# Gate and up projections of a feed-forward layer in seven block products for each pair of weight tiles, with 1/rms moved past the down projection

## The chip, the cores and the metric

The kernel runs on one core of a Trainium2 chip. The metric is the time of one execution on the device, in microseconds; the lower the better.

## What is computed

Two layers of a decoder trunk over 512 positions of width 1024, all in float32. The change touches the second half of each layer, the gated feed-forward (D_FF is 2816), and what follows from it:

```python
h2 = rmsnorm(x, ffn_norm[layer])
gu = jnp.einsum('bsd,df->bsf', h2, w_gate_up[layer])
x = x + jnp.einsum('bsf,fd->bsd', jax.nn.silu(gu[..., :D_FF]) * gu[..., D_FF:], w_down[layer])
```

After the second layer one more `rmsnorm` with `final_norm` gives the output. The first half of each layer (one input projection, three token mixers, their gates and an output projection `w_out`) is not touched.

## The kernel before

**Tiles.** Activations are kept with channels on the 128 partitions and the 512 positions on the free axis, so the layer input is 8 tiles of 128x512 (`KT`). A weight tile of 128x1024 floats holds the 8 blocks of 128x128 that lead from all 1024 input channels to 128 output channels. To keep float32 accuracy each operand is split in a high and a low part (`wh` and `wl` for weights, `hH`, `hL` for activations) and every block takes three matmuls: high with high, high with low, low with high. `fm_tile` (line 343) does one weight tile this way: 8 blocks x 3 = 24 matmuls of 512 columns into one PSUM bank.

**Weights.** `wload` (line 203) brings one weight tile: a DMA of 512 KB on SyncE's queue into `st`, a copy on ScalarE that makes `wh`, a subtraction on VectorE that makes `wl`. `st` has two buffers, `wh` and `wl` three each. Whatever stands under `tc.high_priority()` is put ahead of other ready work on its engine.

**Norm.** `Norm.add` (line 387) takes a finished tile of x while the output projection `w_out` still runs, multiplies it by the norm's gain and splits it; the factor 1/rms per position is only known once all 8 tiles are there. `finish` (line 404) makes it: `rst` with positions on partitions, `rep` the same repeated on all partitions.

**Feed-forward** (lines 1211 to 1247). For each of 22 pairs (`KF`) of a gate tile and an up tile: two `fm_tile`s; VectorE multiplies the gate by `rep`; ScalarE takes silu; GpSimd multiplies by `rep` (for the up half); VectorE multiplies with the up bank; ScalarE copies the high part (`aH`), GpSimd subtracts the low part (`aL`). In layer 0 the down projection then runs tile by tile with `fm_acc`, and VectorE adds each bank to x. In layer 1 `last_down` (line 1259) runs it with positions on partitions and does the final norm; `residual_tm` (line 1249) turns x for that on the side, for 8 of the pairs.

**Order.** TensorE's order is the order of the program, written by hand with generators that `Issue.run` interleaves. Every other engine executes its instructions in the order in which the tile scheduler put them when the kernel was built, and an instruction that waits holds up all that stand behind it on its engine. All instructions are issued by one helper, so they carry one line number (L120 before, L121 in the changed kernel) and are told apart by their tiles.

Of the kernel before, what the change touches and what calls it, by code (L numbers as in the profile page):

```python
# [164 lines left out]
def hybrid_kernel(ctx, tc, x0, pos, wi, wkv, wb, wo, wg, wd, gn, convw, lngb, sguw, sgub,  # L165
# [267 lines left out]
    def layer(l, norm, first=None):  # L433
# [777 lines left out]
        with tc.tile_pool(name=f"ffn{l}", bufs=1, reuse_waits="tile") as fp:  # L1211
            hx = nx.xs
            issue.spawn(0, nx.finish(), nx.accs[0])
            act = []
            for i in range(KF):
                pgt = yield from fm_tile(wg[l, 2 * i], hx)
                pup = yield from fm_tile(wg[l, 2 * i + 1], hx)
                if i == 0:
                    yield f"rep{nx.gi}"
                    rep2 = nx.rep  # L1220
# [7 lines left out]
                nc.scalar.copy(ah, s)  # L1228
                nc.gpsimd.tensor_tensor(al_, s, ah.bitcast(F32), ALU.subtract)
# [183 lines left out]
```

## Time and profile before

| | |
|---|---|
| time, median of 3 runs | 1726.81 us (1724.46 to 1728.25) |
| the profiled execution: its time | 1728.58 us |
| its span, first to last instruction | 1726.5 us |
| mean granted TensorE clock | 0.996 of full speed |
| TensorE matmuls busy | 1706.7 us, 99% of the span |
| VectorE busy | 852.8 us, 49% |
| ScalarE busy | 648.0 us, 38% |
| GpSimd busy | 414.8 us, 24% |
| the chain that ended last | 95% on TensorE |

The rows below come from this profiled execution. Matmuls overlap in the pipeline, so the mean duration of one (389 ns for 512 columns) is not what one adds to the time; the distance from start to start is.

### The profile page before, as it was taken

Reading aid. Unit: us, or ns where it says so; the run is one execution under the profiler, and the core shown is the slowest. Engines: PE = TensorE matmul, PEld = TensorE weight load, DVE = VectorE, ACT = ScalarE, POOL = GpSimd, SP = SyncE. Lnnn points to the kernel's source line nnn. Section 1 sums busy time; section 2 is a strip of 40 time slices with the busy share of each in tenths; the row PEclk is TensorE's granted clock in tenths of the full one; section 3 lists DMA queues with packets and bytes.
Section 4 is the critical chain, followed back from the end, with each engine's and each line's share of the span. In section 5 each row is a group of like instructions: output and inputs, shape, how many; then the busy total and the mean of one; then the engine's idle time right before and its main releaser. Section 6 shows DMA issues by size and latency. Waiting matters only on the chain.

```text
span 1726.5 us, 22439 instructions
## 1 busy us (share of the span) xinstructions
PE 1706.7 (99%) x8580; PEld 1410.4 (82%) x8580; DVE 852.8 (49%) x1624; ACT 648.0 (38%) x1206; POOL 414.8 (24%) x457
## 2 busy tenths in 40 slices
PE   9999999999999999999999999999999999999998
PEld 8888778888888888888888877788888888888886
DVE  7685874544543333323276948644444433333224
ACT  6454663323342222222245546532233322222212
POOL 3423231021223333310024133210212233333000
PEclk9999999999999999999999999999999999999999
DMA  5232112232443223344332220122224534444332
GB/s 163 93 104 90 38 46 96 86 98 90 130 153 99 97 97 98 98 128 125 109 117 98 95 80 26 57 91 91 98 98 134 164 105 120 120 122 158 98 98 85
DMA packets 73116, 176.59 MB, mean 102 GB/s; under 512 B 24945, under 2 KB 25201, under 8 KB 73009
## 3 DMA queue, kind: packets, MB, share of 16 engines
q1 hardware_dynamic: 71184, 170.71, 31.0%
q0 software_dynamic: 1248, 3.41, 0.7%
q8 instruction: 67, 1.10, 0.3%
q10 hardware_dynamic: 576, 1.05, 0.2%
q14 instruction: 41, 0.33, 0.1%
HBM read 162.03 MB, written 13.11 MB: 101 GB/s over the span
## 4 chain that ended last, share of the span: by engine, by line
PE 95%; DVE 2%; ACT 1%; POOL 1%; issue 0%; DMA 0%; SPq 0%; POOLq 0%; ACTq 0%; DVEq 0%
PE mm L120 83%; PE px L120 12%; DVE U L120 0%; DVE wl L120 0%; DMA x<-in_x 0%; ACT pr L120 0%; POOL of L120 0%; DVE xf L120 0%; DVE pr L120 0%; DVE S L120 0%; DVE zg L120 0%; DVE Tc L120 0%; ACT wh L120 0%; POOL pr L120 0%; ACT ojk L120 0%
## 5 line engine op out<-in xcount | busy, mean ns | idle before, releaser
L120 ACT CAST wh<-st 128x1024 fp32r<-128x1024 f32 (+2 forms) x286 | 295.6, 1033 | 815.5 <-PE mm L120 611.0
L120 PE MATMUL mm<-hH,wh 128*128 128x512 f32 x1344 | 532.9, 396 | 0.0
L120 PE MATMUL mm<-hH,wl 128*128 128x512 f32 x1344 | 524.7, 390 | 0.0
L120 PE MATMUL mm<-hL,wh 128*128 128x512 f32 x1344 | 524.1, 390 | 0.0
L120 DVE TENSOR_TENSOR wl<-st,wh 128x1024 fp32r<-128x1024 f32 (+2 forms) x286 | 353.5, 1236 | 226.8 <-ACT wh L120 216.6
L120 PEld LDWEIGHTS mm<-hH,wh 128*128 128x128 f32 x1344 | 253.1, 188 | 53.2 <-issue 2.7
L120 PEld LDWEIGHTS mm<-hH,wl 128*128 128x128 f32 x1344 | 252.8, 188 | 53.3
L120 PEld LDWEIGHTS mm<-hL,wh 128*128 128x128 f32 x1344 | 253.2, 188 | 51.2 <-issue 1.2
L120 POOL TENSOR_TENSOR s<-s,rep 128x512 f32<-128x512 f32 x44 | 77.5, 1762 | 162.1 <-ACT s L120 162.1
L120 POOL TENSOR_TENSOR aL<-s,aH 128x512 fp32r<-128x512 f32 x44 | 77.6, 1764 | 156.3 <-ACT aH L120 152.6
L120 POOL TENSOR_TENSOR gt<-gt,gt 128x512 f32<-128x512 f32 x32 | 48.8, 1524 | 267.8 <-DVE gt L120 267.8
L120 DVE TENSOR_TENSOR s<-mm,s 128x512 f32<-128x512 f32 x44 | 30.4, 692 | 143.6 <-PE mm L120 136.8
L120 DVE TENSOR_TENSOR s<-mm,rep 128x512 f32<-128x512 f32 x44 | 30.4, 692 | 138.2 <-PE mm L120 111.2
L120 DVE TENSOR_TENSOR gt<-mm,rep 128x512 f32<-128x512 f32 x48 | 33.1, 690 | 107.5 <-PE mm L120 107.5
L120 PE MATMUL mm<-wh,hH 128*128 128x512 f32 (+1 forms) x208 | 83.2, 400 | 0.8 <-ACT hH L120 0.8
L120 PE MATMUL mm<-wh,hL 128*128 128x512 f32 (+1 forms) x208 | 79.9, 384 | 0.7 <-DVE hL L120 0.7
L120 PE MATMUL mm<-wl,hH 128*128 128x512 f32 (+1 forms) x208 | 79.5, 382 | 0.0
L120 PE MATMUL mm<-brH,wh 128*128 128x512 f32 x192 | 74.7, 389 | 0.0
L120 PE MATMUL mm<-brL,wh 128*128 128x512 f32 x192 | 74.7, 389 | 0.0
L120 PE MATMUL mm<-brH,wl 128*128 128x512 f32 x192 | 74.7, 389 | 0.0
L120 PE MATMUL mm<-aH,wh 128*128 128x512 f32 x176 | 68.5, 389 | 0.0
L120 PE MATMUL mm<-aL,wh 128*128 128x512 f32 x176 | 68.5, 389 | 0.0
(290 smaller groups left out, 2446.2 us busy)
## 6 DMA issues: line engine op xcount, KB each, us to landing
st<-in_wi SPq DMA_DIRECT2D x104, 512.0 KB, 3.3
st<-in_wg SPq DMA_DIRECT2D x88, 512.0 KB, 3.4
st<-in_wb SPq DMA_DIRECT2D x24, 512.0 KB, 3.4
st<-in_wt SPq DMA_DIRECT2D x22, 512.0 KB, 3.3
st<-in_wo SPq DMA_DIRECT2D x16, 512.0 KB, 3.6
st<-in_wd SPq DMA_DIRECT2D x16, 512.0 KB, 3.5
xscr<-xt SPq DMA_DIRECT2D x24, 256.0 KB, 2.0
xt<-xscr SPq DMA_DIRECT2D x24, 256.0 KB, 2.8
```

The source lines that it names most:

```text
L120: return f(*args, **kw)
```

## The change

The gate and up tiles of a pair are taken together as a 2x2 block matrix: rows are gate and up, columns are the first and the last four input blocks (`a11`, `a12` of the gate tile `ga`, `a21`, `a22` of the up tile `up`, each 128x512). The activations are cut the same way, into channel halves (tiles 0 to 3, tiles 4 to 7) and position halves of 256 (`HT`). Strassen's scheme in Winograd's form then needs seven products of blocks instead of eight, and sums of blocks before and after.

- **`NormSeven`** keeps the split activations and makes three sums (`T2`, `T3`, `-T4`) for the four pairs of tiles (k and k + 4), and one (`T1`) in place; each is split in high and low parts. All that happens while `w_out` runs.
- **`gate_up`** loads the two weight tiles (even pairs into `st`, odd ones into `stx`), forms sums of weight blocks in place (two on GpSimd, two on VectorE), splits four operands (`gate`, `s1`, `s3a22`, `s2s4`), and issues seven products, P1 to P7, of 4 blocks x 3 matmuls of 256 columns. The results are put together by adds of 128x256 on VectorE and GpSimd.
- **1/rms**: the gate is still multiplied by `rep` for silu; the up half is not. Instead the down projection's output is multiplied: by `rep` in layer 0 (one more VectorE instruction per tile), by `rst` within the add in `last_down`.

The core of the diff:

```diff
+        with tc.high_priority():
+            pool, tag = (wst, "st") if i % 2 == 0 else (fw, "stx")
+            ga, up = (pool.tile([P, 1024], F32, tag=tag, name=nm("st"), bufs=2) for _ in range(2))
+            nc.sync.dma_start(ga, wg[l, 2 * i])
+            nc.sync.dma_start(up, wg[l, 2 * i + 1])
+            a11, a12, a21, a22 = ga[:, :HK], ga[:, HK:], up[:, :HK], up[:, HK:]
...
+            s1 = fw.tile([P, HK], F32, tag="s1", name=nm("s1"))
+            nc.gpsimd.tensor_tensor(s1, a21, a22, ALU.add)
+            gate = split(ga, wst, "wh", "wl", None)
+            nc.gpsimd.tensor_tensor(a21, a11, a21, ALU.subtract)
+            sum1 = split(s1, fw, "s1h", "s1l", 1)
+            s3a22 = split(up, wst, "wh", "wl", None)
+            nc.vector.tensor_tensor(a11, s1, a11, ALU.subtract)
+            nc.vector.tensor_tensor(a12, a12, a11, ALU.subtract)
+            s2s4 = split(ga, wst, "wh", "wl", None)
...
+        def product(ps, w, j, x):
+            wh, wl = w
+            for k, (xh, xl) in enumerate(nx.operand(x)):
+                sl = slice((4 * j + k) * P, (4 * j + k + 1) * P)
+                nc.tensor.matmul(ps, lhsT=wh[:, sl], rhs=xh, start=k == 0, stop=False)
+                nc.tensor.matmul(ps, lhsT=wh[:, sl], rhs=xl, start=False, stop=False)
+                nc.tensor.matmul(ps, lhsT=wl[:, sl], rhs=xh, start=False, stop=k == 3)
+            yield
+
+        add = nc.vector.tensor_tensor, nc.gpsimd.tensor_tensor
+        yield from product(b12[:, lo_], gate, 0, "B11")
+        nc.scalar.copy(g[:, lo_], b12[:, lo_])
+        yield from product(b57[:, lo_], sum1, 0, "T1")
+        yield from product(b12[:, hi_], gate, 1, "B21")
+        yield from product(b57[:, hi_], s3a22, 0, "T3")
+        nc.scalar.copy(t, b57)
+        yield from product(b63[:, lo_], s2s4, 0, "T2")
+        add[0](g[:, hi_], b63[:, lo_], g[:, lo_], ALU.add)
+        add[0](g[:, lo_], b12[:, hi_], g[:, lo_], ALU.add)
+        add[1](t[:, lo_], t[:, lo_], g[:, hi_], ALU.add)
+        add[1](u[:, hi_], t[:, lo_], t[:, hi_], ALU.add)
+        add[1](t[:, hi_], t[:, hi_], g[:, hi_], ALU.add)
+        yield from product(b63[:, hi_], s2s4, 1, "B22")
+        yield from product(b4[:, lo_], s3a22, 1, "-T4")
+        add[0](g[:, hi_], b63[:, hi_], t[:, lo_], ALU.add)
+        add[0](u[:, lo_], b4[:, lo_], t[:, hi_], ALU.add)
...
-                s = rot("s")
-                nc.vector.tensor_tensor(s, pgt, rep2, ALU.mult)
-                nc.scalar.activation(s, s, AF.Silu)
-                nc.gpsimd.tensor_tensor(s, s, rep2, ALU.mult)
-                nc.vector.tensor_tensor(s, pup, s, ALU.mult)
...
+                nc.vector.tensor_tensor(g, g, nx.rep, ALU.mult)
+                nc.scalar.activation(g, g, AF.Silu)
+                nc.vector.tensor_tensor(g, g, u, ALU.mult)
...
-                nc.vector.tensor_tensor(xt, pd, xt, ALU.add)
+                pr = rot("pr")
+                nc.vector.tensor_tensor(pr, pd, nx.rep, ALU.mult)
+                nc.vector.tensor_tensor(xt, pr, xt, ALU.add)
```

**How the order changes.** The first place is the middle of layer 0's loop over pairs, on VectorE. Before, two pairs (four weight tiles; `s` is the gate, then the product):

```order
L120 TENSOR_TENSOR s_970_5161<-mm_962_5099,rep_914_4795 128x512
L120 TENSOR_TENSOR wl_980_5204<-st_978_5202,wh_979_5203 128x1024
L120 TENSOR_TENSOR s_970_5161<-mm_966_5130,s_970_5161 128x512
L120 TENSOR_TENSOR wl_987_5244<-st_985_5242,wh_986_5243 128x1024
L120 TENSOR_TENSOR s_981_5232<-mm_973_5170,rep_914_4795 128x512
L120 TENSOR_TENSOR wl_991_5275<-st_989_5273,wh_990_5274 128x1024
L120 TENSOR_TENSOR s_981_5232<-mm_977_5201,s_981_5232 128x512
L120 TENSOR_TENSOR wl_998_5315<-st_996_5313,wh_997_5314 128x1024
```

In the changed kernel, one pair: tiles g_1022, t_1023 and u_1024 belong to the pair whose products run; st_1027 and st_1028 (its gate and up tile), s1_1029 and wl_1031 to wl_1037 to the weights of the next pair:

```order
L121 TENSOR_TENSOR wl_1033_5486<-s1_1029_5478,wh_1032_5485 128x512
L121 TENSOR_TENSOR wl_1031_5481<-st_1027_5474,wh_1030_5480 128x1024
L121 TENSOR_TENSOR st_1027_5474<-s1_1029_5478,st_1027_5474 128x512
L121 TENSOR_TENSOR st_1027_5474<-st_1027_5474 128x512
L121 TENSOR_TENSOR g_1022_5371<-mm_1020_5369,g_1022_5371 128x256
L121 TENSOR_TENSOR g_1022_5371<-mm_1018_5367,g_1022_5371 128x256
L121 TENSOR_TENSOR g_1022_5371<-mm_1020_5369,t_1023_5372 128x256
L121 TENSOR_TENSOR g_1022_5371<-g_1022_5371,rep_944_4923 128x512
L121 TENSOR_TENSOR wl_1035_5490<-st_1028_5475,wh_1034_5489 128x1024
L121 TENSOR_TENSOR u_1024_5373<-mm_1021_5370,t_1023_5372 128x256
L121 TENSOR_TENSOR g_1022_5371<-g_1022_5371,u_1024_5373 128x512
L121 TENSOR_TENSOR wl_1037_5496<-st_1027_5474,wh_1036_5495 128x1024
```

Four instructions of a pair have become twelve, and those of the next pair's weights stand between those of this pair's results. Below they are called D1 to D12 in this order.

The same place on GpSimd; before, two pairs:

```order
L120 TENSOR_TENSOR s_970_5161<-s_970_5161,rep_914_4795 128x512
L120 TENSOR_TENSOR aL_972_5167<-s_970_5161,aH_971_5166 128x512
L120 TENSOR_TENSOR s_981_5232<-s_981_5232,rep_914_4795 128x512
L120 TENSOR_TENSOR aL_983_5238<-s_981_5232,aH_982_5237 128x512
L120 TENSOR_TENSOR s_992_5303<-s_992_5303,rep_914_4795 128x512
```

and in the changed kernel one pair, where s1_1049 and st_1048 are the weights of the pair after the next:

```order
L121 TENSOR_TENSOR s1_1049_5610<-st_1048_5607 128x512
L121 TENSOR_TENSOR st_1048_5607<-st_1047_5606,st_1048_5607 128x512
L121 TENSOR_TENSOR t_1023_5372<-t_1023_5372,g_1022_5371 128x256
L121 TENSOR_TENSOR u_1024_5373<-t_1023_5372 128x256
L121 TENSOR_TENSOR t_1023_5372<-t_1023_5372,g_1022_5371 128x256
L121 TENSOR_TENSOR aL_1026_5471<-g_1022_5371,aH_1025_5470 128x512
```

Two instructions of a pair have become six, Q1 to Q6 below; the two sums for weights two pairs ahead stand in front of the three adds that this pair's result needs.

The second place is the same stretch of the loop on ScalarE. Before, one pair and a half:

```order
L120 ACTIVATE s_970_5161<-s_970_5161 128x512
L120 CAST wh_986_5243<-st_985_5242 128x1024
L120 CAST aH_971_5166<-s_970_5161 128x512
L120 CAST wh_990_5274<-st_989_5273 128x1024
L120 ACTIVATE s_981_5232<-s_981_5232 128x512
L120 CAST wh_997_5314<-st_996_5313 128x1024
```

and in the changed kernel one pair, from the copy of this pair's high part aH to the one of the next:

```order
L121 CAST aH_1025_5470<-g_1022_5371 128x512
L121 CAST wh_1052_5617<-s1_1049_5610 128x512
L121 CAST wh_1050_5612<-st_1047_5606 128x1024
L121 COPY t_1043_5504<-px_1039_5500 128x512
L121 CAST wh_1054_5621<-st_1048_5607 128x1024
L121 ACTIVATE g_1042_5503<-g_1042_5503 128x512
L121 CAST wh_1056_5627<-st_1047_5606 128x1024
```

The casts of the weights two pairs on (wh_1052, wh_1050) now stand behind the cast aH_1025, the end of this pair's result.

The third place is the start of layer 0's feed-forward on VectorE. Before, from the last tile of x on:

```order
L120 TENSOR_TENSOR xt_897_4714<-mm_893_4683,xt_897_4714 128x512
L120 TENSOR_TENSOR wl_921_4818<-st_919_4816,wh_920_4817 128x1024
L120 SCALAR_TENSOR_TENSOR hL_899_4719<-xt_897_4714,gnt_75,hH_898_4718 128x512
L120 TENSOR_TENSOR sq_844_4429<-sq_844_4429,sq_900_4722 128x512
L120 TENSOR_SCALAR ms_906_4765<-px_905_4760 128x4
```

and in the changed kernel, behind the same last tile (xt_913), where st_921 and wl_927 to wl_931 are the first pair's weights and st_947, wl_951 and wl_953 the second's:

```order
L121 SCALAR_TENSOR_TENSOR hL_915_4775<-xt_913_4770,gnt_75,hH_914_4774 128x512
L121 SCALAR_TENSOR_TENSOR t4_917_4779<-xt_913_4770,gnt_75,t23_916_4778 128x256
L121 TENSOR_TENSOR x2_919_4784<-t23_916_4778,x2_918_4783 128x512
L121 TENSOR_TENSOR x2_919_4784<-t4_917_4779,x2_918_4783 128x256
L121 TENSOR_TENSOR sq_845_4437<-sq_845_4437,sq_920_4789 128x512
L121 TENSOR_TENSOR st_921_4799<-s1_923_4803,st_921_4799 128x512
L121 TENSOR_TENSOR wl_927_4811<-s1_923_4803,wh_926_4810 128x512
L121 TENSOR_TENSOR wl_929_4815<-st_922_4800,wh_928_4814 128x1024
L121 TENSOR_TENSOR st_921_4799<-st_921_4799 128x512
L121 TENSOR_TENSOR wl_931_4821<-st_921_4799,wh_930_4820 128x1024
L121 TENSOR_TENSOR wl_951_4953<-st_947_4946,wh_950_4952 128x1024
L121 TENSOR_TENSOR wl_953_4958<-s1_949_4950,wh_952_4957 128x512
```

The sums and the splits of the first pair's weights, its gate tile apart, stand behind the last norm tile.

## Rows read from the trace of the kernel before

**Rows 1.** Part 1 of the page: busy time, share, instructions of each engine.

```profile
PE 1706.7 (99%) x8580; PEld 1410.4 (82%) x8580; DVE 852.8 (49%) x1624; ACT 648.0 (38%) x1206; POOL 414.8 (24%) x457
```

**Rows 2.** Busy time by window, layer 0's feed-forward: PE, PEld, DVE, ACT, POOL; granted clock.

```profile
512.00:744.00 232.00, 232.00 (x1025) 192.08 (x1024) 82.55 (x87) 71.12 (x89) 75.91 (x44) 1.00 0.30 98
```

**Rows 3.** The chain that ended last: start, length, engine and tile, instructions.

```profile
862.86 2.19 PE px L120 x18
...
1121.75 10.89 PE mm L120 x48
```

**Rows 4.** The timeline, layer 0's loop: start, length, engine, instruction, idle before it.

```profile
639.92 0.63 ACT L120 ACTIVATE s<-s 128x512 f32<-128x512 f32 x1
640.04 1.23 DVE L120 TENSOR_TENSOR wl<-st,wh 128x1024 fp32r<-128x1024 f32 x1 [0.21 <-ACT wh L120]
640.63 1.78 POOL L120 TENSOR_TENSOR s<-s,rep 128x512 f32<-128x512 f32 x1 [3.66 <-ACT s L120]
```

**Rows 5.** Groups by form: count | busy us, mean ns of one | idle before.

```profile
L120 DVE TENSOR_TENSOR sq<-sq,sq 128x512 f32<-128x512 f32 x10 | 6.9, 686 | 0.1
L120 DVE TENSOR_TENSOR U<-px,U 128x256 f32<-128x256 f32 x12 | 5.1, 421 | 0.2
L120 DVE SCALAR_TENSOR_TENSOR hL<-xt,gnt,hH 128x512 fp32r<-128x512 f32 x24 | 17.9, 747 | 0.2 <-ACT hH L120 0.2
L120 ACT CAST wh<-st 128x1024 fp32r<-128x1024 f32 x270 | 283.8, 1051 | 776.2 <-PE mm L120 578.0 <-issue 106.5 <-PE px L120 88.4
L120 ACT CAST aH<-s 128x512 fp32r<-128x512 f32 x44 | 27.4, 622 | 2.5 <-DVE s L120 2.4
L120 ACT COPY pT<-px 128x512 f32<-128x512 f32 x24 | 13.7, 580 | 6.8 <-PE px L120 6.7
L120 ACT COPY aq<-px 128x256 f32<-128x256 f32 x16 | 5.8, 365 | 10.4 <-PE px L120 10.3
L120 POOL TENSOR_TENSOR la<-la,tri_le 128x256 f32<-128x256 f32 x16 | 13.4, 855 | 4.1 <-ACT la L120 4.1
```

**Rows 6.** The timeline, GpSimd alone: 512 columns, and twice 256 columns.

```profile
59.37 1.43 POOL L120 TENSOR_TENSOR la<-la,tri_le 128x256 f32<-128x256 f32 x2
434.88 1.29 POOL L120 TENSOR_TENSOR gt<-gt,gt 128x512 f32<-128x512 f32 x1 [3.86 <-DVE gt L120]
```

**Rows 7.** The timeline where VectorE and GpSimd work at the same time.

```profile
235.97 1.28 POOL L120 TENSOR_TENSOR wsT<-wsT,tri_le 128x512 f32<-128x512 f32 x1 [0.49 <-DMA wsT<-in_sguw]
...
236.04 0.42 DVE L120 TENSOR_TENSOR U<-px,U 128x256 f32<-128x256 f32 x1
...
393.30 1.28 POOL L120 TENSOR_TENSOR gt<-gt,gt 128x512 f32<-128x512 f32 x1 [6.88 <-DVE gt L120]
...
393.32 2.34 DVE L120 TENSOR_TENSOR wl<-st,wh 128x1024 fp32r<-128x1024 f32 x1
...
442.28 1.23 DVE L120 TENSOR_TENSOR wl<-st,wh 128x1024 fp32r<-128x1024 f32 x1
442.33 2.33 POOL L120 TENSOR_TENSOR gt<-gt,gt 128x512 f32<-128x512 f32 x1 [6.16 <-DVE gt L120]
```

**Rows 8.** The timeline, VectorE with two instructions back to back.

```profile
432.93 1.22 DVE L120 TENSOR_TENSOR wl<-st,wh 128x1024 fp32r<-128x1024 f32 x1
434.06 0.68 DVE L120 SCALAR_TENSOR_TENSOR gt<-gt,mm 128x512 f32<-128x512 f32 x1
```

**Rows 9.** Busy time by window round an idle TensorE in layer 1.

```profile
1066.00:1068.00 2.00, 0.00 (x0) 0.00 (x0) 1.46 (x7) 0.00 (x0) 0.70 (x1) 1.00 0.00 0
...
1070.00:1072.00 2.00, 2.00 (x7) 1.55 (x6) 1.46 (x10) 1.64 (x8) 0.61 (x1) 0.54 0.00 0
1072.00:1074.00 2.00, 2.00 (x14) 1.25 (x13) 1.22 (x10) 1.09 (x4) 1.81 (x4) 0.61 0.00 0
1074.00:1076.00 2.00, 2.00 (x17) 1.67 (x16) 0.33 (x2) 1.33 (x5) 0.06 (x1) 1.00 0.01 4
```

**Rows 10.** DMA issues: count, KB each, us from issue to landing.

```profile
st<-in_wg SPq DMA_DIRECT2D x88, 512.0 KB, 3.4
```

More of the change, by code (lines that the diff above doesn't have):

```diff
@@ L30 @@
 H = 64
+HT = T // 2
 CI_QKV, CI_U, CI_Q, CI_V, CI_Z, CI_G = 0, 12, 16, 20, 24, 28
@@ L1196, in layer @@
             ms_.append((mh, ml_))
-        nx = Norm(2 * l + 1)
+        fx = tc.tile_pool(name=f"fx{l}", bufs=1, reuse_waits="tile", side="right")
+        nx = NormSeven(2 * l + 1, fx.__enter__())
         xold = x0 if l == 0 else xscr
@@ L1211, in layer @@
         with tc.tile_pool(name=f"ffn{l}", bufs=1, reuse_waits="tile") as fp:
[L1212 removed]
             issue.spawn(0, nx.finish(), nx.accs[0])
             act = []
+            fwp = tc.tile_pool(name=f"fw{l}", bufs=1, reuse_waits="tile")
+            fw = fwp.__enter__()
             for i in range(KF):
[L1216 to L1217 removed]
+                g, u = yield from gate_up(l, i, nx, fw)
                 if i == 0:
                     yield f"rep{nx.gi}"
[L1220 to L1225 removed]
+                nc.vector.tensor_tensor(g, g, nx.rep, ALU.mult)
+                nc.scalar.activation(g, g, AF.Silu)
+                nc.vector.tensor_tensor(g, g, u, ALU.mult)
                 ah = fp.tile([P, T], F32R, tag=f"aH{i}", name=nm("aH"))
                 al_ = fp.tile([P, T], F32R, tag=f"aL{i}", name=nm("aL"))
[L1228 to L1229 removed]
+                nc.scalar.copy(ah, g)
+                nc.gpsimd.tensor_tensor(al_, g, ah.bitcast(F32), ALU.subtract)
                 act.append((ah, al_))
@@ L1232, in layer @@
                     residual_tm((i - 4) // 2)
+            fwp.__exit__(None, None, None)
+            fx.__exit__(None, None, None)
             if last:
-                yield from last_down(fp, act)
+                with tc.tile_pool(name="end", bufs=1, reuse_waits="tile") as ep:
+                    yield from last_down(ep, act, nx.rst)
                 return None
@@ L1247, in layer, with gate_up, split @@
         return nn
+    def gate_up(l, i, nx, fw):
+        HK = KT // 2 * P
+        issue.ahead = True
+        with tc.high_priority():
[4 more added lines that the diff above has]
+            a11, a12, a21, a22 = ga[:, :HK], ga[:, HK:], up[:, :HK], up[:, HK:]
+            def split(st, pool, th, tl, bufs):
+                hi = pool.tile(list(st.shape), F32R, tag=th, name=nm("wh"), bufs=bufs)
+                lo = pool.tile(list(st.shape), F32R, tag=tl, name=nm("wl"), bufs=bufs)
+                nc.scalar.copy(hi, st)
+                nc.vector.tensor_tensor(lo, st, hi.bitcast(F32), ALU.subtract)
+                return hi, lo
+            s1 = fw.tile([P, HK], F32, tag="s1", name=nm("s1"))
[7 more added lines that the diff above has]
+            s2s4 = split(ga, wst, "wh", "wl", None)
+        issue.ahead = False
+        tag = "px" if i % 2 else "mm"
+        yield max(issue.bank_free(tag, 4 - n) - 1.4 * n for n in range(4))
+        b12, b57, b63, b4 = (bank(tag) if i % 2 else mm_bank() for _ in range(4))
+        g, t, u = rot("g"), rot("t"), fw.tile([P, T], F32, tag="u", name=nm("u"), bufs=2)
+        lo_, hi_ = slice(0, HT), slice(HT, T)
+        def product(ps, w, j, x):
[23 more added lines that the diff above has]
+        add[0](u[:, lo_], b4[:, lo_], t[:, hi_], ALU.add)
+        return g, u
@@ L1257, in residual_tm, with last_down @@
                               xb[32 * a:32 * a + 32, :].rearrange("i (b j) -> i b j", j=32))
-    def last_down(fp, act):
+    def last_down(ep, act, rst):
         xs_, fin = [], []
-        gft = fp.tile([P, D], F32, name="gft")
+        gft = ep.tile([P, D], F32, name="gft")
         nc.sync.dma_start(gft, gf)
         for c in range(NCH):
-            xt = fp.tile([P, D], F32, tag=f"xf{c}", name=nm("xf"))
+            xt = ep.tile([P, D], F32, tag=f"xf{c}", name=nm("xf"))
             nc.sync.dma_start(xt, xtok[c * P:(c + 1) * P, :])
@@ L1294, in last_down @@
                 sl = slice(h * 512, (h + 1) * 512)
-                nc.vector.tensor_tensor(xt[:, sl], banks[c][h], xt[:, sl], ALU.add)
+                nc.vector.scalar_tensor_tensor(xt[:, sl], banks[c][h], rst[:, c:c + 1], xt[:, sl],
+                                               ALU.mult, ALU.add)
                 sq = rot("sq")
```

39 lines of the change are left out of this document (added).

## The prediction

> **What bounds the kernel now.** I read the page's busy times first: TensorE's matmuls fill 99% of the span, no other engine half of it [rows 1]. Then the window of layer 0's feed-forward: TensorE 232 of 232 us, VectorE 83, ScalarE 71, GpSimd 76, full clock [rows 2]. So that stage is TensorE's, and the others wait for it. What one matmul costs is read from the chain, where pieces without a gap stand as one: 48 matmuls of 512 columns in 10.89 us, 226.9 ns each; 18 of 264 columns in 2.19 us, 121.7 ns each [rows 3]. The 48 are one pair of tiles, so the feed-forward before takes 22 x 10.89 = 239.6 us in each layer up to its down projection.
>
> **What the change removes and adds on TensorE.** A pair has 7 x 4 x 3 = 84 matmuls of 256 columns in place of 48 of 512. From the two rows a column costs (226.9 - 121.7) / 248 = 0.424 ns, so 256 columns cost 118.3 ns; if the weight load sets the 264-column row, it stays at 121.7. I take 118.3, eight columns from a row: a product is 12 x 118.3 = 1.42 us, a pair 9.94 us (at most 10.22). If TensorE stayed the bound, 0.95 us a pair would be won. The Trainium skill (TensorE: Matmul & The Clock Gate, Back-to-back issue gap) gives N / 2.4 + 2.5 ns, by which 256 columns cost 109 ns and a pair 9.2 us; at 264 columns it gives 112.5 where the row has 121.7, so the row decides.
>
> **What it adds elsewhere.** Durations: VectorE 512 columns 0.69, 256 columns 0.42 [rows 5], 1024 columns 1.23 [rows 4]; ScalarE 1.05 for 1024, 0.62 for 512, 0.58 and 0.36 from PSUM for 512 and 256 [rows 5]; GpSimd alone 1.29 for 512 and 0.72 for 256 columns [rows 6], up to 0.86 as a mean [rows 5]. Per pair VectorE has three splits of 1024, five instructions of 512, four of 256: 3.69 + 3.45 + 1.68 = 8.8 us. ScalarE has 3 x 1.05 + 0.62 + 0.63 + 0.62 + 0.58 + 0.36 = 6.0, GpSimd 3 x 1.29 + 3 x 0.72 = 6.0. Each alone fits into 9.94. Two things in the rows say that together they don't.
>
> First, **VectorE and GpSimd exclude each other** when both read two operands from SBUF. GpSimd's product that starts 0.05 us into a split ends 1.15 us after the split's end and so takes 2.33 in place of 1.29; a split that starts 0.02 into GpSimd's product takes 2.34 in place of 1.23, ending 1.08 after it [rows 7]. A VectorE instruction with one operand in PSUM runs beside GpSimd at its usual 0.42 [rows 7]. Of VectorE's twelve, D1 to D4, D8, D9, D11 and D12 have two SBUF operands; all six of GpSimd's do. Back to back an instruction starts 0.09 before the end of the one ahead [rows 8]: 5 x 0.60 + 3 x 1.14 = 6.4 for VectorE, 3 x 1.15 + 3 x 0.58 = 5.2 for GpSimd: 11.6 us a pair if not a moment is lost, more than the 10.89 before.
>
> Second, **the order makes a ring**. With D and Q numbered as in the section on the change, D3 is the last reader of s1, which has one buffer; Q1, the next s1, waits for it. Q2 follows Q1, Q3 to Q5 stand behind both. D7 overwrites the half of g that Q5 reads and waits for it. D8 to D11 follow on VectorE, aH on ScalarE waits for D11, and behind aH stand the casts of the weights two pairs on (s1's, then the gate's). D2 waits for that gate cast, and D3 for D2. This closes once per pair, without TensorE. Walked with 0.08 us from engine to engine (silu's end to GpSimd's start [rows 4]) and an estimated 0.04 between dependent instructions of one engine: D3 ends at 0.69, D4 at 1.42; Q1, held by D4, at 2.57; Q2 3.9; Q3, Q4, Q5 at 4.65, 5.4, 6.2; D7 6.7; D8 7.4; D9 8.5; D10 8.9; D11 9.6; aH 10.3; s1's cast 10.8; gate cast 11.8. Meanwhile D12 ends at 10.7, Q6 (behind aH and D12) at 11.9, D1 behind Q6 at 12.4, D2 at 13.6, and there the next D3 starts. **A period is 13.6 us.** Without any collision D4 and Q6 drop out: 12.6. Without the steps from one instruction to the next either: 12.15. Upwards: GpSimd's 256 columns at the mean of 0.86 add 0.4, late weight DMAs some 0.3 (the second tile's DMA can go when D12 of two pairs before is done, 10.7, and lands 3.4 later [rows 10], at 14.1, where Q1 would want it at 13.6 + 0.8), one more collision 0.3: 14.6. I take 13.6, since every step in it stands in a row. The Trainium skill (SBUF — State Buffer, two separate sides) says that whichever starts first holds the shared port pair for its whole instruction and the other blocks fully. By that the loser runs its full 1.29 after the wait where the rows have 1.15; with three hand-overs in the ring the period would be 14.0 and the total 17 us higher.
>
> **Where TensorE then stands.** P4 needs D9 (0.24 after its start): 8.3 after D3; P5 needs D12: 10.5. P1 to P3 end at 5.4, so TensorE idles 2.9 us before P4 and 0.8 before P5, 3.7 us a pair.
>
> **Start and end of a stage.** The first pair's a11 sum and s1 split stand behind the last norm tile. From the last matmul of w_out on, VectorE has the add to x, the gain sums, splits and the square (0.69 + 2 x 0.42 + 0.75 + 0.42 + 0.69 + 0.42 + 0.69 = 4.5; the 0.75 from [rows 5]), the first pair's 0.69 + 0.69 + 1.23 + 0.69 + 1.23, a wait of about 1 for ScalarE's last cast, then 1.23 and 0.69 for the second pair: its D3 starts at about 11.5, some 1 us saved back to back. P2 of the first pair so waits 4.2 us. From there 20 periods to the last pair's D3, and from that 10.5 + 3 x 1.42 = 14.8 to its last product: 11.5 + 20 x 13.6 + 14.8 = 298.3 us, against 239.6: **58.7 us lost in each layer**.
>
> **The rest costs nothing or little.** Norm tiles 4 to 7 put 4.6 us on VectorE and 1.15 on GpSimd into the 24 x 0.227 = 5.45 us of one w_out tile: TensorE covers that, by little; 0 to 2 us a layer. The multiplication by rep in layer 0's down projection is 0.69 per tile beside 66 x 0.227 = 15 us of matmuls. The scaling in the last adds makes 0.69 into 0.75: 0.1 us at the end. GpSimd's product by rep goes, but it was covered. Layer 1's transposes of x stand between D6 and D7, where VectorE waits from 2.4 to 6.2; the same wait covers what they cost.
>
> **Sum.** 1728.6 (this execution) + 2 x 58.7 = 1846; the median of the runs lies 1.8 lower: **1844 us**.
>
> **Rivals.** (a) *TensorE stays the bound*: GpSimd and VectorE run ahead and the ring hides. 22 x 9.94 + 4.2 = 222.9, 16.7 won per layer: 1693. For it: every engine's sum is under 9.94. Against: the ring would have to be 3.7 us shorter, though only 1 of it is collisions. 6%. (b) *No net change*: a period of 10.9 by shorter GpSimd times; 1727; the ring without collisions and steps is 12.15. 3%. (c) *The exclusion alone binds*: waits overlap better than I walked and the period is 11.6 to 12.1: 11.5 + 20 x 11.6 + 14.8 = 258.3 gives 1764, 12.1 gives 1784. It decides if Q1 doesn't wait for D3 or D7 not for Q5. 13%. (d) *The clock falls with the gaps*: an idle TensorE of over 2 us was followed by 0.54 and 0.61 of full clock for some 4 us, then full [rows 9]. Here such a gap comes in each pair; half speed for 3.4 us costs 1.7 us, within the 3.7 that TensorE idles, so 3 us in all at the two ends. Only with half clock throughout does TensorE bind: 84 x 0.237 = 19.9 us a pair, 2120 us. 3%.
>
> **How the numbers follow.** The forecast, a period of 12.15 to 14.6, gives 1784 to 1884, and to 1892 with the norm tiles and the clock at the ends: 75%. The range takes in the upper half of (c): 1775 to 1892 holds about 80%. Faster is (a), 6%; within 0.2%, about what a measurement of this kernel can tell from no change, is (b), 3%; slower the rest, 91%.
>
> **What would show it.** In the profile after: TensorE idle some 3.7 us a pair in the feed-forward, waiting for VectorE's wl, most of it before P4; pairs 13.6 us apart; sums on GpSimd of 512 columns longer than 1.29 beside VectorE; matmuls of 256 columns 118 ns apart; the rest of the kernel as before. I am wrong if matmuls stand back to back across pairs, if Q1 starts before D3 ends, or if VectorE's and GpSimd's busy time overlap freely.

## The result, and the profile after

The changed kernel takes **1872.2 us** (median of 4 runs, 1869.9 to 1873.7) where the kernel before takes 1725.6 beside it: a ratio of 1.0849, 95% interval 1.0836 to 1.0863. The forecast was 1844 in a range of 1775 to 1892. So the side and the range held, and the loss, 147 us, is some 29 us larger than the 117 that the sum gave.

Part 1 of the page, profiled execution of 1872.35 us (span 1870.7); it answers to [rows 1]:

```profile
PE 1710.8 (91%) x10164; PEld 1478.7 (79%) x10164; DVE 1133.4 (61%) x2032; ACT 769.0 (41%) x1414; POOL 549.0 (29%) x641
```

TensorE's busy time is 4 us longer than before, its share fell from 99% to 91%. By window (us, then busy time and count of PE, PEld, DVE, ACT, POOL; clock, DMA share, GB/s), first the stretch of [rows 2], then 19 pairs of layer 0 and one of them:

```profile
512.00:744.00 232.00, 179.76 (x1388) 172.41 (x1388) 153.87 (x200) 93.87 (x133) 107.56 (x100) 0.98 0.24 74
614.31:628.08 13.77, 10.59 (x86) 10.19 (x85) 9.33 (x12) 5.67 (x8) 6.30 (x6) 1.00 0.22 76
530.46:796.96 266.50, 207.10 (x1602) 199.40 (x1600) 177.52 (x228) 107.52 (x152) 122.19 (x114) 0.97 0.25 76
```

TensorE worked 232 of 232 us in this stretch before and now works 180. Nobody else is full: VectorE 66%, GpSimd 46%. The loss lies wholly in the two feed-forwards: from the first matmul behind `w_out` to the first matmul of the down projection layer 0 takes 315.3 us (497.4 to 812.7 in the trace) where it took 241.2, layer 1 takes 314.9 where it took 241.2. `w_out` (43.5 us) and layer 0's down projection (119.7 us) take as long as before.

One pair of the loop, from one D3 to the next. The timeline of the kernel after: start, length, engine, instruction, idle before it and who ended it. VectorE (D3, D4, D5 with D6, D7 to D12, D1, D2, D3):

```profile
614.31 0.69 DVE L121 TENSOR_TENSOR st<-s,st 128x512 f32<-128x512 f32 x1
615.03 0.69 DVE L121 TENSOR_TENSOR st<-st 128x512 f32<-128x512 f32 x1
615.64 0.88 DVE L121 TENSOR_TENSOR g<-px,g 128x256 f32<-128x256 f32 x2
620.65 0.43 DVE L121 TENSOR_TENSOR g<-px,t 128x256 f32<-128x256 f32 x1 [4.13 <-POOL t L121]
...
623.99 1.22 DVE L121 TENSOR_TENSOR wl<-st,wh 128x1024 fp32r<-128x1024 f32 x1
625.28 1.63 DVE L121 TENSOR_TENSOR wl<-s,wh 128x512 fp32r<-128x512 f32 x1
626.83 1.21 DVE L121 TENSOR_TENSOR wl<-st,wh 128x1024 fp32r<-128x1024 f32 x1
628.08 0.69 DVE L121 TENSOR_TENSOR st<-s,st 128x512 f32<-128x512 f32 x1
```

GpSimd (Q1 to Q6), and of ScalarE the cast aH and the two weight casts behind it:

```profile
615.64 1.28 POOL L121 TENSOR_TENSOR s<-st 128x512 f32<-128x512 f32 x1 [3.05 <-DMA st<-in_wg]
617.00 1.30 POOL L121 TENSOR_TENSOR st<-st,st 128x512 f32<-128x512 f32 x1
618.25 0.74 POOL L121 TENSOR_TENSOR t<-t,g 128x256 f32<-128x256 f32 x1
619.07 0.73 POOL L121 TENSOR_TENSOR u<-t 128x256 f32<-128x256 f32 x1
619.88 0.73 POOL L121 TENSOR_TENSOR t<-t,g 128x256 f32<-128x256 f32 x1
624.80 1.56 POOL L121 TENSOR_TENSOR aL<-g,aH 128x512 fp32r<-128x512 f32 x1 [4.18 <-ACT aH L121]
...
624.10 0.62 ACT L121 CAST aH<-g 128x512 fp32r<-128x512 f32 x1 [0.43 <-DVE g L121]
624.63 0.62 ACT L121 CAST wh<-s 128x512 fp32r<-128x512 f32 x1
625.39 1.05 ACT L121 CAST wh<-st 128x1024 fp32r<-128x1024 f32 x1
```

This is the ring as it was walked: Q1 at the end of D4, Q2 to Q5 without a gap, D7 as soon as Q5 is done (VectorE has stood idle for 4.13 us by then), then VectorE without a pause from D8 to D12, D1 (made longer by Q6 beside it), D2 and the next D3. The cast aH and the two weight casts behind it end at 626.44, 0.4 us before D2 begins, so in this pair they hold nothing up. The ring takes 13.77 us. But the row of Q1 names a DMA: there is a **second way round of the same length**. The chain that ended last, read for this stretch (start, length, what), goes over it:

```profile
610.22 1.23 DVE wl L121
611.46 4.02 DMA st<-in_wg
...
615.64 1.28 POOL s L121
```

D12 frees the gate tile's buffer, the DMA for two pairs later is issued and lands 4.0 us on, Q1 starts. Whichever of the two is late by a little closes the ring. What the profile can't tell is whether the ring makes the 13.7 us, or whether VectorE and GpSimd, which exclude each other, would take as long in any order. The runs were made for that.

### The profile page after: what moved, and what is told of

It reads as the page before. It is cut to its first block, busy times and chain, and to the rows that moved or that the text cites. A ratio compares the mean times of both kernels' runs of the same rounds, so it can differ in the third digit from the quotient of the medians.

```text
span 1870.7 us, 26663 instructions
## 1 busy us (share of the span) xinstructions
PE 1710.8 (91%) x10164; PEld 1478.7 (79%) x10164; DVE 1133.4 (61%) x2032; ACT 769.0 (41%) x1414; POOL 549.0 (29%) x641
## 4 chain that ended last, share of the span: by engine, by line
PE 64%; DVE 12%; POOL 10%; DMA 6%; issue 5%; ACT 3%; POOLq 0%; SPq 0%; DVEq 0%; ACTq 0%
PE mm L121 51%; PE px L121 13%; DMA st<-in_wg 5%; DVE wl L121 5%; POOL t L121 3%; POOL st L121 3%; POOL s L121 2%; DVE g L121 2%; POOL u L121 1%; ACT wh L121 1%; DVE st L121 1%; ACT g L121 1%; DVE hL L121 1%; DVE xf L121 0%; DVE x L121 0%
## 5 line engine op out<-in xcount | busy, mean ns | idle before, releaser
L121 PE MATMUL mm<-hH,wh 128*128 128x512 f32 (+1 forms) x992 | 365.4, 368 | 72.9 <-ACT g L121 33.3
L121 PE MATMUL mm<-hH,wl 128*128 128x512 f32 (+1 forms) x992 | 353.9, 357 | 2.2 <-DVE wl L121 2.2
L121 PE MATMUL mm<-hL,wh 128*128 128x512 f32 (+1 forms) x992 | 353.0, 356 | 0.0
L121 PE MATMUL px<-hH,wh 128*128 128x256 f32 x352 | 105.0, 298 | 64.7 <-ACT g L121 34.4
L121 POOL TENSOR_TENSOR gt<-gt,gt 128x512 f32<-128x512 f32 x32 | 48.8, 1524 | 267.8 <-DVE gt L121 267.8
L121 PE MATMUL mm<-x,wh 128*128 128x256 f32 x528 | 103.3, 295 | 0.0
L121 PE MATMUL px<-hH,wl 128*128 128x256 f32 x352 | 100.4, 285 | 0.0
L121 PE MATMUL px<-hL,wh 128*128 128x256 f32 x352 | 100.4, 285 | 0.0
L121 PE MATMUL px<-x,wh 128*128 128x256 f32 x528 | 98.8, 287 | 0.0
L121 PEld LDWEIGHTS mm<-x,wh 128*128 128x128 f32 x528 | 87.9, 204 | 0.7 <-issue 0.7
L121 PEld LDWEIGHTS px<-x,wh 128*128 128x128 f32 x528 | 84.2, 196 | 0.0
```

What stands on the lines that cost most here:

```text
L121: return f(*args, **kw)
```

## The experiments

A ratio is against the kernel before, run beside it (1723.1 to 1724.9 us).

### TensorE's waits: two bank halves exchanged (e1)

Where TensorE waits wasn't what was forecast: not for the weights of P4 and P5 but before P3 and P6, 1.59 us each, for VectorE's or ScalarE's `g`. The first matmul of P6, and of the next pair's P3:

```profile
616.12 0.39 PE L121 MATMUL px<-hH,wh 128*128 128x256 f32 x1 [1.59 <-DVE g L121]
...
623.73 0.39 PE L121 MATMUL mm<-hH,wh 128*128 128x256 f32 x1 [1.59 <-ACT g L121]
```

P3 goes into the second half of the bank in whose first half P1's result stands until ScalarE has copied it, P6 into that of P5's. Here P3 and P6 exchange places, so that neither follows its bank's first product so closely.

```diff
-        yield from product(b12[:, hi_], gate, 1, "B21")
+        yield from product(b26[:, lo_], gate, 1, "B21")
...
-        yield from product(b63[:, hi_], s2s4, 1, "B22")
+        yield from product(b13[:, hi_], s2s4, 1, "B22")
```

> P2 and P6 share a PSUM bank here, and P1 and P3, so that TensorE no longer waits in a pair for a copy or an add that reads the other half of the bank it writes; everything else is computed as before, though ScalarE and VectorE get their instructions of a pair in a slightly other order. Theory A (the ring over VectorE, GpSimd and ScalarE sets 13.7 us a pair, TensorE only follows it): the two gaps of 1.6 us before P3 and P6 go, but the same 3 to 4 us stand before other products; the period stays between 13.3 and 13.8 us, the time between 1853 and 1876 us. Theory B (TensorE's waits for the two bank neighbours are the loss, as the table of its waits names them): the period falls by 3.2 us to 10.6, 42 pairs give 134 us, the time is about 1738 us.

Measured: 1855.67 us, 1.0763 [1.0747, 1.0779]. TensorE's waits (who, for whom: us in all, times, longest), after and in this run:

```profile
PE px L121 <- ACT g L121: 34.4, 20, 3.4
PE mm L121 <- ACT g L121: 33.3, 20, 2.6
PE px L121 <- DVE g L121: 30.3, 22, 1.9
PE mm L121 <- DVE g L121: 29.9, 21, 3.2
```

```profile
PE px L121 <- DVE wl L121: 45.6, 19, 3.4
PE mm L121 <- DVE wl L121: 42.5, 21, 3.4
```

The 128 us of waits for `g` are gone, and 88 us for `wl` stand in their place, before P4, where the prediction had put most of them. The period stays: 19 periods of layer 0 take 260.7 us, 13.72 each, nearly all 13.78. What was won, some 15 us, is that single long periods (below) are gone and the first ones are shorter. TensorE's waits show the length of an undisturbed period, they don't make it; for the long ones see the last of the wrong terms below.

### The ring's waits, one by one (e2, e3, e4, e5)

e2 gives `s1` two buffers, and `u` one in place of two (Q1 no longer waits for D3); e3 gives the weight tiles of a third pair a buffer in space that the activations of the last two pairs use later (the DMA no longer waits for D12 of two pairs before); e4 does both; e5 does both and keeps Q1 from being put ahead of Q6 of three pairs before.

```diff
-            s1 = fw.tile([P, HK], F32, tag="s1", name=nm("s1"))
+            s1 = fw.tile([P, HK], F32, tag="s1", name=nm("s1"), bufs=2)
...
+            if i % 3 == 2 and i < KF - 4:
+                ga, up = (fp.tile([P, 1024], F32, tag=f"act{KF - 2 + j}", name=nm("st")) for j in range(2))
```

> s1 gets two buffers (and u one in place of two), so Q1 no longer waits for D3. Theory A1 (the ring closes through D3 alone, as predicted): Q1 starts right behind Q6, the period falls from 14.0 on average to 11.6 to 12.1 us, 40 periods give 76 to 96 us: 1776 to 1796 us. Theory A2 (a second ring of the same length closes through the reload: D12, the last reader of a weight buffer, 1.23; its DMA 4.0; Q1, Q2 and the three adds 5.1; D7 to D11 3.4: 13.8 us): the period stays within 0.3 us of 13.8, the time between 1860 and 1874 us.

> The weight tiles of a pair get a third set of buffers for the first 18 pairs of a layer (in the places of the last two pairs' results), so that a reload does not wait for the pair before; s1 keeps one buffer. Theory A1 or A2 (the ring through D3 stands by itself): the typical period stays at 13.7 us, and only the pairs above it (15 to 17 us, some two or three a layer) can become shorter: 1860 to 1873 us. A theory in which the DMA alone sets the period: 11.6 to 12.1 us, 1776 to 1796 us.

> Both edits together: two buffers for s1 and a third set of weight tiles. Theory A2: only now both ways from the weights back to Q1 are open. What is left is a ring through GpSimd's own order (Q6, Q1 to Q5, then D7 to D11 and aH on the other engines, then Q6 again: 6.4 + 4.1 = 10.5 us) and the exclusion of VectorE and GpSimd (11.6 us if nothing is lost): a period of 11.6 to 12.3 us, and with 40 periods at 1.7 to 2.4 us less 1776 to 1804 us. Theory B (TensorE's bank waits): no change, 1865 to 1875 us.

> As the fourth run (two buffers for s1, a third set of weight tiles), but Q1 of a pair is held at its old place in GpSimd's order, two pairs ahead (there the greedy order had taken it a third pair ahead, behind the very reader of s1 that it should no longer meet). Now Q1 meets neither D3 nor a late reload. Theory A2 (these two waits are the loss): the period falls to what is left of waits between engines, 11.3 us; the time is about 1765 us. Theory C (VectorE and GpSimd are one resource, since they exclude each other, and the rings are full only because it is: VectorE's twelve instructions take some 8.3 us in a row, GpSimd's six some 5.4, in sum 13.7, and the order lets hardly any of it overlap): the period stays at 13.7 us, the time between 1865 and 1880 us, and GpSimd's Q1 and Q2 now stand longer than 1.29 us each, beside VectorE's D2 and D3.

Measured: e2 1870.0 (1.0840 [1.0817, 1.0863]), e3 1867.35 (1.0827 [1.0811, 1.0843]), e4 1872.77 (1.0864 [1.0847, 1.0880]), e5 1880.07 (1.0892 [1.0876, 1.0909]). None shortens the period: it is mostly 13.7 us in e2 and e3, 13.7 to 14.1 in e4. What Q1 waits for, one row each of GpSimd's timeline in e2, e3 and e4:

```profile
616.87 1.76 POOL L121 TENSOR_TENSOR s<-st 128x512 f32<-128x512 f32 x1 [2.51 <-DMA st<-in_wg]
```

```profile
614.42 1.73 POOL L121 TENSOR_TENSOR s<-st 128x512 f32<-128x512 f32 x1 [2.54 <-issue]
```

```profile
604.91 1.28 POOL L121 TENSOR_TENSOR s<-st 128x512 f32<-128x512 f32 x1 [3.24 <-DVE st L121]
```

Without the `s1` wait it is the DMA; with a third pair of weight buffers it is again the end of D3 (here 613.59 + 0.69); and with both the scheduler, which issues what is ready, took the added buffers to put Q1 a pair further ahead, so that it stands behind a D3 once more. In e5 Q1 and Q2 start at last right behind Q6, and run beside VectorE's splits:

```profile
614.22 1.57 POOL L121 TENSOR_TENSOR aL<-g,aH 128x512 fp32r<-128x512 f32 x1 [4.18 <-ACT aH L121]
615.73 1.75 POOL L121 TENSOR_TENSOR s<-st 128x512 f32<-128x512 f32 x1
617.56 2.12 POOL L121 TENSOR_TENSOR st<-st,st 128x512 f32<-128x512 f32 x1
621.44 0.73 POOL L121 TENSOR_TENSOR t<-t,g 128x256 f32<-128x256 f32 x1 [1.75 <-DVE g L121]
```

Each is longer by a collision (1.75 and 2.12 for 1.29), so is VectorE's work beside them, and then the two wait for each other in turn. The period is mostly 13.8 to 15.3. From this I read at the time (theory C in the texts of e5 to e7) that the two engines need 13.7 us in turn in any order. e11, run last, shows that this reading was wrong.

### The order alone (e11)

The sums, their engines and the PSUM banks of the changed kernel stay; `s1` has two buffers and `u` one, as in e2. What each engine issues is written out as one list per pair (wrapped here) and held to it, TensorE's products included; +1 is the next pair, -1 the one before. `s2`, `s4`, `U2`, `C11`, `C12`, `D8`, `s3L`, `ulo`, `D11`, `s24L`, `s1L`, `gateL` are D3 to D12, D1, D2; `s1`, `s3`, `Q3`, `Q4`, `Q5`, `aL` are Q1 to Q6.

```diff
+    ORDER7 = """s3+1 P4 gateH+1 C11-1 P5 s1L+1 C12-1 D8-1 gC ldB+2 U2 gateL+1 P7 tC s2+1 P2+1 P1+1
+        silu-1 ldA+2 P6 s3H+1 ulo-1 Q3 s1+2 s4+1 D11-1 s3L+1 s24H+1 s24L+1 s1H+2 Q4 aH-1 Q5 aL-1 P3+1""".split()
```

> The sums of the changed kernel as they are (Q1 to Q6 on GpSimd, D1 to D12 on VectorE, the same PSUM banks, s1 in two buffers, u in one); only the order on VectorE, GpSimd, ScalarE and TensorE is written out by hand, so that a pair's casts stand ahead of the aH of the pair before, and the adds of a pair's results no longer close a ring with the next pair's sums. Theory O (the order of the queues makes 13.7 us of the 11.6 that exclusion alone asks for): a period of 11.3 to 11.7 us, a feed-forward of 262 to 274 us per layer, 1755 to 1790 in all. Theory X (VectorE and GpSimd lose 2 us a pair to each other in any order, so 13.7 is what the exclusion costs): a period of 13.5 to 14 us and 1850 to 1880.

Measured: **1754.91 us**, 1.0176 [1.0159, 1.0193]: theory O. Against e2, which has the same buffers and the scheduler's order, the ratios differ by 0.0664: the order alone gives back some 115 of the 147 us lost. Layer 0's loop by window:

```profile
540.00:740.00 200.00, 191.20 (x1484) 180.64 (x1483) 197.54 (x213) 97.23 (x143) 175.27 (x106) 1.00 0.30 92
```

and two of GpSimd's groups in it (count | busy us, mean ns | idle):

```profile
L121 POOL TENSOR_TENSOR t<-t,g 128x256 f32<-128x256 f32 x36 | 59.5, 1654 | 1.4
L121 POOL TENSOR_TENSOR s<-st 128x512 f32<-128x512 f32 x18 | 31.3, 1739 | 0.0
```

The period is 11.34 us. VectorE is busy for 197.5 of 200 us, GpSimd for 175, and nearly every GpSimd instruction collides: an add of 256 columns takes 1.65 us where it takes 0.73 after, a sum of 512 columns 1.74. Yet the loop is 2.4 us a pair shorter. The difference is that Q3, Q4 and Q5 now have most of a period before C12 (D7) asks for them, since the sums and splits of the next pair's weights stand between on VectorE; after, VectorE did nothing for 4.13 us there. VectorE has hardly any idle time left in this order, and the period is close to the 11.6 that the prediction had worked out from the exclusion; whether another order with the same instructions would be shorter still was not tried. TensorE's products stand in another order here too; that this is not what shortened the period rests on e1, where TensorE's waits changed place and the period stayed.

### Fewer instructions that exclude each other (e6, e7)

e6 leaves the scheduler its order and moves Q1, Q2 and Q6 to VectorE. e7 leaves them, but adds Q3 to Q5 on VectorE straight from P2's and P4's bank, without ScalarE's copy `t`, so that P5 goes ahead of P4. The adds of e7:

```diff
-        add[1](t[:, lo_], t[:, lo_], g[:, hi_], ALU.add)
-        add[1](u[:, hi_], t[:, lo_], t[:, hi_], ALU.add)
-        add[1](t[:, hi_], t[:, hi_], g[:, hi_], ALU.add)
+        add[0](t[:, lo_], b57[:, lo_], g[:, hi_], ALU.add)
+        add[0](t[:, hi_], b57[:, hi_], g[:, hi_], ALU.add)
+        add[0](u[:, hi_], b57[:, lo_], t[:, hi_], ALU.add)
```

> Q1, Q2 and Q6, the three sums of 512 columns, go from GpSimd to VectorE; buffers as in the changed kernel. VectorE gets 2 us more work per pair, 10.9 us, GpSimd keeps the three adds of 256 columns. Theory C: each of the three takes about 0.6 us of the shared resource in place of 1.3, so the period falls by 2.1 us to 11.6, and the time to 1772 to 1792 us, though the busier of the two engines got the work. A theory in which the chain of waits alone counts (Q1 and Q2 lie on it, Q6 doesn't): 1.4 us less, 12.3 us a pair, 1800 to 1810 us. A theory in which VectorE's own work is the bound: 13.7 + 1.8 = 15.5 us a pair, 1940 us.

> Q3, Q4 and Q5, the three adds of 256 columns on GpSimd, become three adds on VectorE with one operand read straight from PSUM (ScalarE's copy of that bank goes; P5 is issued ahead of P4). Q1, Q2 and Q6 stay on GpSimd, buffers stay. VectorE gets three instructions of 0.42 us more, GpSimd 2.3 us less. Theory C: an instruction with an operand in PSUM can run beside GpSimd, so the shared resource loses 2.4 us and gains nothing or little: a period of 11.0 to 11.5 us, 1752 to 1776 us. Theory A2 without exclusion: the waits for s1 and for the reload stay and only their adds get shorter, 12.6 us: 1812 us.

Measured: e6 1817.03 (1.0538 [1.0519, 1.0556]), outside what was expected; e7 1756.71 (1.0183 [1.0169, 1.0197]). e6 has its 11.56 us a pair in layer 0 and loses it in layer 1, where the periods are 12.3 to 17.1 us. The longest, and in it the wait of P6 for U2 (D5) and that of D7 for P6:

```profile
1476.42:1493.50 17.08, 12.84 (x86) 12.64 (x86) 10.96 (x16) 5.87 (x8) 2.19 (x3) 0.80 0.37 102
```

```profile
1481.22 0.58 PE L121 MATMUL mm<-hH,wh 128*128 128x256 f32 x1 [4.24 <-DVE g L121]
...
1484.29 0.42 DVE L121 TENSOR_TENSOR g<-mm,t 128x256 f32<-128x256 f32 x1 [2.20 <-PE mm L121]
```

In layer 0 the scheduler put U2 right behind D3; in layer 1 two or three sums for the next weights stand ahead of it, and here one of them waits for its weight DMA (4.93 us to landing). P6 waits 1.8 to 4.2 us for U2 in layer 1 (from 1409 to 1524 us), 1.2 to 1.5 in layer 0 (584 to 608). In most of these periods TensorE's clock then falls to half, and D7 has to wait for a slow P6. In the period from 1464.12 on, with a wait of 1.83 us, the clock stayed at 1.00 and the period is 12.3. How much is due to the order and how much to the clock was not tried apart.

e7 has a period of 11.13 in layer 0 and 11.13 to 11.28 in layer 1: the three adds no longer exclude GpSimd, and GpSimd's part of the ring is gone. That e7 and e6's layer 0 came out as theory C had sized them doesn't save it, since both edits shorten the ring as well.

### The move of 1/rms alone (e8)

The kernel before, without GpSimd's multiplication by `rep`, with the scaling behind the down projection in both layers.

```diff
-                nc.gpsimd.tensor_tensor(s, s, rep2, ALU.mult)
...
-                nc.vector.tensor_tensor(xt, pd, xt, ALU.add)
+                pr = rot("pr")
+                nc.vector.tensor_tensor(pr, pd, nx.rep, ALU.mult)
+                nc.vector.tensor_tensor(xt, pr, xt, ALU.add)
```

> The kernel before with the other half of the change alone: the up half is no longer multiplied by rep on GpSimd, the down projection's output is (layer 0: one more VectorE instruction of 0.69 us per tile; layer 1: within the last add). By the prediction TensorE covers all of it: 1724 to 1728 us, a ratio of 0.998 to 1.002. If the multiplication on GpSimd had been on the path it would be faster by some of 44 x 1.8 us; if the additions wait at the end of a down tile, slower by up to 8 x 0.7 = 5.6 us.

Measured: 1725.38, 1.0002 [0.9993, 1.0011]. GpSimd's busy time falls from 414.8 to 338.2 us and nothing comes of it; both halves of this edit were covered, as forecast.

### Both at once: adds from PSUM and a written order (e9, e10)

All seven sums of results are taken from PSUM on VectorE (`U2`, `C11`, `U3`, `U4`, `C12`, `uhi`, `ulo`), tile `u` goes, `s1` has two buffers, the products are spread differently over the PSUM banks, and the order is written out, another one in each run. In e9 Q1 is on VectorE, in e10 on GpSimd. The order of e9 (wrapped here):

```diff
+    ORDER7 = """P7 ulo-1 gC s1L P4 silu-1 ldB+2 ldA+2 D11-1 s3+1 s3H+1 gateL+1 P5 P6 aH-1 U2 C11 U3 s2+1
+        P2 s3L+1 P3+1 s1H+1 s1+2 s4+1 U4 C12 uhi P1+1 aL-1 s24H+1 gateH+2 s24L+1 D8""".split()
```

> The seven products with all seven sums of their results read from PSUM on VectorE (no bank copied but P1's, no tile u), Q1 on VectorE, Q2 and Q6 on GpSimd, two buffers for s1, and the order of every engine in the loop written by hand: weights one to two pairs ahead, VectorE's instructions with an operand in PSUM where GpSimd works. Theory C: of the shared resource only VectorE's work with two SBUF operands (7.0 us) and two GpSimd sums (2.3 us) are left, 9.3 us, less than TensorE's 7 x 1.42 = 9.94, so TensorE binds: a period of 9.95 to 10.1 us, the first pair still late by some 7.5 us in each layer, 22 x 10.0 + 7.5 = 227.5 in place of 241.3 us: 1695 to 1706 us, faster than the kernel before. If TensorE's waits were the true cost of so many small products, the period stays above 10.9 us and the time above 1727 us.

> As the run beside it with Q1, Q2 and Q6 all left on GpSimd, as in the changed kernel, and an order of its own. VectorE's work with two SBUF operands 6.4 us, GpSimd's three sums 3.45 us, in sum 9.85: just under TensorE's 9.94. Theory C: still TensorE-bound if nothing is lost, 10.0 to 10.4 us a pair, 1697 to 1722 us. Without the exclusion the two runs are the same within 2 us.

Measured: e9 **1711.08 us**, 0.9912 [0.9898, 0.9927], faster than both kernels, if 5 us behind what was expected; e10 1727.74, 1.0019 [1.0007, 1.0030], 0.2% behind the kernel before and 6 us outside. Since the two differ in their order as well, the 17 us between them can't be put down to Q1's engine. Layer 0 of e9 by window, from shortly behind `w_out` on, and from the timeline TensorE's one wait there:

```profile
502.00:504.00 2.00, 0.00 (x0) 0.00 (x0) 2.00 (x5) 0.00 (x0) 0.25 (x1) 0.63 0.99 385
504.00:512.00 8.00, 7.14 (x33) 7.14 (x34) 4.38 (x7) 3.15 (x4) 4.57 (x3) 0.50 0.27 80
...
600.00:650.00 50.00, 50.00 (x419) 50.00 (x418) 49.44 (x81) 25.99 (x35) 14.62 (x10) 1.00 0.34 106
```

```profile
504.86 0.58 PE L121 MATMUL mm<-hH,wl 128*128 128x256 f32 x1 [5.80 <-DVE wl L121]
```

From there on TensorE has no gap in layer 0: a matmul starts every 0.120 us, and the period is 10.08 us in place of 10.89. Of the 22 x 0.81 = 17.8 us that this gives, 9.7 go at the start of the layer, whose feed-forward takes 233.1 us in place of 241.2: 5.8 us of waiting for the first pair's weights, which stand on VectorE behind the last norm tile, and then half clock (1.2 in place of 2.4 GHz) for 8 us, in which matmuls of 256 columns start every 0.213 us (25 of the 33; the other 8 have one column). Mending this start wasn't tried.

## Why the prediction was right, and where it wasn't

**Right: the limit and the ring.** The period was forecast as 13.6 and is 13.7 to 13.8 where nothing disturbs it, by the steps that were walked. Collisions have the size that [rows 7] gave: Q6 starts while D12 runs, ends 1.15 us after it, and takes 1.56; D1 beside it takes 1.63 in place of 0.69. So the trace stays with the rows and not with the reading of the Trainium skill's page (SBUF — State Buffer, two separate sides) by which the loser would still need its full 1.29. TensorE's 256 columns are 120.0 ns apart against 118.3 forecast. The norm and 1/rms cost `w_out` and the down projection nothing, which e8 shows for 1/rms.

**Rival (c), the exclusion alone**, was priced at 1764 to 1784 with 13%, to hold if Q1 doesn't wait for D3 or D7 not for Q5. e11 is that case: same sums, 1754.9, with a period of 11.34 where 11.6 was taken. Its first condition was not enough: e2 to e5 took Q1's waits away and gained nothing, because another wait of equal length stood behind each. The second was: e11 puts work between Q5 and D7, e7 takes GpSimd out of it. So the ring is D7's wait for GpSimd with all that queues behind it, and it is a matter of order, not of the sum of the work. That the order sets the period is shown by e2 and e11; that this wait is the link that counts is read from the 4.13 us of the trace, since e7 and e11 each change more than this link.

**Wrong: where TensorE waits.** Forecast were 2.9 us before P4 and 0.8 before P5; there are 1.59 before P3 and 1.59 before P6. The sum is near (3.2 for 3.7), the place isn't: that a product waits for the reader of the *other half* of its bank was missing. The Trainium skill has that rule (PSUM — Partial Sum Buffer, PSUM bank collisions raise a hardware error): guard by bank, not by address. The waits in e1's table agree with it, though a bank is one tile in this kernel, so they can't tell a guard by bank from one by tile. The undisturbed period didn't suffer by it, as e1 shows, since the ring closes elsewhere; the long periods did (below).

**Wrong: four terms of the sum**, together 17.0 us a layer (298.3 forecast, 315.3 measured in layer 0), counted from the end of `w_out`. The feed-forward before was taken as 239.6 and is 241.2, so the loss was put 15.4 us a layer too small, which makes up about the 29 us.

- The second pair's D3 comes after 15.9 us, not 11.5 (the terms listed for it add up to 11.0 with the saving). VectorE was late with the norm's sums of the tile before, beside GpSimd's first sums for the weights: the first row below holds two subtractions, of 512 and of 256 columns, that take 1.02 us together a tile later and here take 3.18, so that the last tile's add begins 2.7 us late. The prediction had looked for this cost in `w_out` (0 to 2 us) and not behind it.

```profile
497.05 3.18 DVE L121 TENSOR_TENSOR x<-t,x 128x512 fp32r<-128x512 f32 x2
500.15 0.68 DVE L121 TENSOR_TENSOR xt<-mm,xt 128x512 f32<-128x512 f32 x1
```

- The next period is 17.1 and not 13.6: it holds the making of 1/rms and `rep`, and a table load of 1.28 us on ScalarE ahead of the first silu, none of which was counted.
- The mean of the other 19 periods is 266.5 / 19 = 14.03 (+8.1 us). Most are 13.7 to 14.0; single ones are 14.6, 15.2 and 16.4. In the longest the chain goes over a weight DMA of 5.84 us where it has about 4.0 elsewhere. The term for late DMAs (0.3 a pair) was on the list of what could lengthen the period and was not taken. In the two longest the clock takes part as well (next paragraph); the rest is not traced to one cause.
- From the last D3 to the last product 15.7 us, not 14.8.

All four erred to the same side. The result lies in the range because its upper end had been set by a longer period (14.6), not because these terms were foreseen. Rival (b) was mispriced too: by the prediction's own sum a period of 10.9 gives 1736, not 1727.

**Rival (d), the clock,** stayed small, but not for the reason given, that half clock fits into TensorE's idle time. In the period of 15.23 us from 585.37 on TensorE stood idle for 2.62 us before P3, and P3 then ran at half clock:

```profile
585.37:600.60 15.23, 11.02 (x77) 10.62 (x77) 9.39 (x12) 5.19 (x8) 6.29 (x6) 0.89 0.24 79
```

```profile
595.81 0.39 PE L121 MATMUL mm<-hH,wh 128*128 128x256 f32 x1 [2.62 <-ACT g L121]
...
597.98 0.41 PE L121 MATMUL mm<-hH,wl 128*128 128x256 f32 x1
...
598.26 1.04 ACT L121 CAST wh<-st 128x1024 fp32r<-128x1024 f32 x1 [0.93 <-ACT wh L121]
```

ScalarE's cast of the next gate tile goes into the buffer that P3 reads, and it starts when P3's last matmul is done. D2 waits for that cast and D3 for D2, so a slow P3 lies on the ring: from D7 to the next D3 it takes 7.86 us here and 8.21 in the period of 16.37 us (clock 0.81), where the pair shown above has 7.43. That is 0.4 and 0.8 us; the rest of the excess is a late Q1 in both. e1, in which P3 doesn't wait, has no period over 13.81 us among its 19. At half clock 256 columns are 0.213 us apart, not the 0.237 that the rival took.

## What to carry to other kernels

When two engines each fit into the period alone, add up what they can't do at the same time, and then look for the ring: which instruction waits for the other engine's last result, and what is queued behind it. Taking single waits out of such a ring, or adding buffers, brought nothing here; an order that puts other work between a request to the other engine and the use of its answer brought some 115 of 147 us with the same instructions. Saving TensorE one product in eight at the price of some twice the work on VectorE and GpSimd together paid in one of the versions tried, e9, whose adds take operands from PSUM and whose order leaves TensorE no gap, and there by 0.9%.
